# Row sums of the spatial mixing weights: a VectorE reduction with a store and a spreading load in place of a TensorE product with ones

## The chip, the cores and the metric

The kernel runs on one core of one Trainium2 chip. The metric is the device time of one execution in microseconds (us), the median of several. A core has TensorE (PE in the profile; its weight loads are PEld), VectorE (DVE), ScalarE (ACT), GpSimd (POOL) and SyncE (SP), which issues most DMAs. Each works through its own instructions in a fixed order and waits for the others by semaphores.

## The reference, cut to what matters

One layer of a hybrid encoder over 512 tokens of width 1024, all in float32. The part that the change touches is the spatial gating: a layer norm of `zv`, whose gain and bias are `ln_g` and `ln_b`, is mixed over the 128 positions of each chunk by one 128x128 matrix per head.

```
def sgu_branch(zu, zv, ln_g, ln_b, w_s, bias):        # w_s (8, 128, 128), bias (8, 128)
    zu = gelu(zu)
    zv = layer_norm(gelu(zv), ln_g, ln_b)
    zv = zv.reshape(bsz, seq // 128, 128, 8, 128)
    sv = einsum('hts,bnshd->bnthd', w_s, zv) + bias.T[None, None, :, :, None]
    return zu * sv.reshape(bsz, seq, 1024)
```

Beside it run an S5 state-space branch (a scan over 62 chunks of 8 positions, with small products before and after), gates, a cross-attention and a feed-forward network, all with large products.

With z the normalised `zv` before gain and bias, the mixed value of head h, output position t and channel d is `g[d] * (sum over s of w_s[h,t,s] z[s,d]) + b[d] * R[h,t] + bias[h,t]`, where `R[h,t] = sum over s of w_s[h,t,s]` is the row sum of the mixing weights. These row sums are what the change computes in another way.

## The kernel before, in words

Every large product is made exact to about float32 by splitting each operand into a high and a low part (line 85 on ScalarE, `whi`; line 86 on VectorE, `wlo`) and adding three TensorE products (line 374). Weights arrive in blocks of 512 KB (`wraw`, three buffers, issued on SP's queue at line 145), are split into `whi`/`wlo` (three buffers each), and used. A list (`plan`) names all blocks in order: `next_w` hands out one block, splits up to two blocks ahead and loads three ahead.

Side work is threaded between these products. `tick` is called after each block and moves a counter `side["now"]` by about one per 24 matrix products; `later(n, fn)` runs `fn` when the counter has moved by n; the generator `s5_program` gives the S5 branch piece by piece. The program text so made is then put in order for each engine by a scheduler that models durations, so an edit at one place moves neighbours. What is marked `in_order` keeps its program order; `behind(ins, first)` asks that one instruction comes after another, without a wait of its own.

The stage of the change is the one that makes gate a: eight blocks of `w_in` (four calls of `feat` with `ga_evac`, tiles `pf`). Threaded into it are:

- `layer_norm(t)` (lines 1130 to 1142), four times: mean on VectorE (`nm`), squares on ScalarE into the tile `squares`, the factor on GpSimd, the scaling of `zt` on ScalarE.
- the S5 inputs: VectorE makes a factor (lines 972 to 976) in half of the tile `wsx`, TensorE transposes it (`pw`, line 951), ScalarE copies it (`wt`, line 952), TensorE multiplies by `u` (`pz`, line 958), ScalarE and VectorE keep the result in `zh` (lines 963 and 964). The eighth `pz` is the last thing the scan needs before it starts.
- `s5_scan` (lines 985 to 988): 62 steps of four small VectorE instructions each, every step on the one before. After it, lines 1001 and 1002 copy the states into `ss`, and TensorE multiplies them (`py`, line 1014).
- `mixing_setup` (lines 1151 to 1169): TensorE transposes the mixing weights (`wsr`, which were loaded at line 1144) into `pws`, ScalarE copies them into `wst`; gain and bias are transposed into `pgb` and copied into `gbc`; then TensorE multiplies a matrix of ones by `wst` (line 1164), which puts the row sums of every head on all 128 partitions of `prs`, and eight VectorE instructions (line 1167) turn `mix`, which holds the bias, into `R * b + bias`.

After the stage come the mixing products `psv` (line 1191), whose evacuation (line 1192) reads `gbc` and `mix`, and then the blocks of `zu`, of gate b and the products that follow.

`wsx` holds four parts: `wsr`, `wst`, and the two factors of the S5 inputs. `squares` has four rows of 1024 for each partition, one for each token tile.

Of the kernel before, what the change touches and what calls it, by code (L numbers as in the profile page):

```python
# [9 lines left out]
F32 = mybir.dt.float32  # L10
F32R = mybir.dt.float32r
AF = mybir.ActivationFunctionType
ALU = mybir.AluOpType
AX = mybir.AxisListType
# [3 lines left out]
P = 128  # L18
# [11 lines left out]
H = 8  # L30
# [6 lines left out]
OFF_GA = OFF_V + GW  # L37
# [15 lines left out]
def hybrid_layer_kernel(  # L53
# [8 lines left out]
    nc = tc.nc  # L62
# [9 lines left out]
    dp = ctx.enter_context(tc.tile_pool(name="scratch", bufs=1, space=DRAM))  # L72
# [4 lines left out]
    def bank(name):  # L77
        return pm.tile([P, 512], F32, tag="mm", name=name)

    def aux(name, shape=(P, 512)):  # L80
        return pa.tile(list(shape), F32, tag="aux", name=name)
# [35 lines left out]
    def behind(ins, first):  # L117

        tc.add_manual_dep(ins.ins, first.ins.name, mybir.DependencyInfo(
            mybir.DependencyClass.NoSync, mybir.DependencyReason.DATA), reason="order of the casts")  # L120
# [336 lines left out]
    def later(n, fn):  # L457

        side["later"].append((side["now"] + n, fn))
# [32 lines left out]
    ones = cp.tile([P, P], F32, name="ones")  # L492
# [4 lines left out]
    def sum_sq(dst, src, sq=None, bias=0.0):  # L497
        if sq is None:
            sq = np_.tile([P, 512], F32, tag="ev", name="sq", bufs=2)
        act = nc.scalar.activation(sq[:, :src.shape[-1]], src, AF.Square, bias=bias, accum_out=dst)  # L500
        if pinned[0]:
            in_order(act)
# [11 lines left out]
    HALF = (slice(0, 512), slice(512, 1024))  # L514
# [39 lines left out]
    def slot(tag, shape, dt, name, place=NEAR):  # L554
        n = math.prod(shape[1:])
        t = sp.tile([P, KD * T + ROOM[tag]], dt, tag=tag, name=name)[:, place[tag]:place[tag] + n]
        return t.rearrange("p (a b c) -> p a b c", a=shape[1], b=shape[2]) if len(shape) == 4 else (
            t.rearrange("p (a b) -> p a b", a=shape[1]))
# [526 lines left out]
    zsum = cp.tile([P, NT, 2], F32, name="zsum")  # L1085
# [8 lines left out]
    wsr, wst = wsx[:, 0], wsx[:, 1]  # L1094
# [32 lines left out]

    squares = slot("A", (P, NT, GW), F32, "squares")

    def layer_norm(t):  # L1130

        nm, ss, ms, r = (np_.tile([P, 1 + (k == "ss")], F32, tag=k, name=k, bufs=2) for k in ("nm", "ss", "ms", "r"))
        nc.vector.tensor_tensor(nm, zsum[:, t, 0:1], zsum[:, t, 1:2], ALU.add)
        nc.vector.tensor_scalar(nm, nm, -1.0 / GW, None, ALU.mult)
        z = zt[:, t, :]
        for i in range(2):
            sum_sq(ss[:, i:i + 1], z[:, HALF[i]], squares[:, t, HALF[i]], nm)
        nc.vector.tensor_tensor(ms, ss[:, 0:1], ss[:, 1:2], ALU.add)
        nc.vector.tensor_scalar(ms, ms, 1.0 / GW, EPS, ALU.mult, ALU.add)
        nc.gpsimd.tensor_tensor(r, ms, mhalf, ALU.pow)  # L1140
        nc.vector.tensor_tensor(nm, nm, r, ALU.mult)
        nc.scalar.activation(z, z, AF.Identity, bias=nm, scale=r)
# [5 lines left out]
    mix = np_.tile([P, H, P], F32, tag="gain", name="mix", bufs=2)  # L1148
    nc.sync.dma_start(mix, sgu_bias[0].rearrange("h t -> (h t)").partition_broadcast(P))

    def mixing_setup():
        for q in range(2):
            ps = aux("pws", (P, 4, P))
            for j in range(4):
                nc.tensor.transpose(ps[:, j, :], wsr[:, 4 * q + j, :], ident)
            nc.scalar.copy(wst[:, 4 * q:4 * q + 4, :], ps)
        ps = aux("pgb", (P, 2 * H))
        nc.tensor.transpose(ps, gbr, ident[:2 * H, :2 * H])
        gbc = np_.tile([P, 2 * H], F32, tag="gbc", name="gbc", bufs=1)
        nc.vector.tensor_copy(gbc, ps)  # L1160

        for q in range(2):
            ps = aux("prs", (P, 4, P))
            nc.tensor.matmul(ps, ones, wst[:, 4 * q:4 * q + 4, :], start=True, stop=True)
            for j in range(4):
                h_ = 4 * q + j
                nc.vector.scalar_tensor_tensor(mix[:, h_, :], ps[:, j, :], gbc[:, H + h_:H + h_ + 1], mix[:, h_, :],
                                               ALU.mult, ALU.add)
        return gbc

    gad = dp.tile([KD, P, T], F32, name="gad")

    def ga_evac(m, j, ps):
        z = np_.tile([P, T], F32, tag="ev", name="gas", bufs=2)
        nc.scalar.activation(z, ps, AF.Sigmoid)
        nc.sync.dma_start(gad[m - OFF_GA // P], z)

    gbcs = []
    later(5, lambda: gbcs.append(mixing_setup()))
    for i in range(NT):  # L1180
        later(1 + i, lambda i=i: layer_norm(i))
    for c0 in range(OFF_GA, OFF_GB, 256):
        feat(w_in, c0, xn, KD, ga_evac)


    gbc = gbcs[0]
    sv = slot("A", (P, H, T), F32, "sv")
    for h in range(H):
        ps = bank("psv")
# [56 lines left out]
    def unit_bank(name):  # L1246
        return bank(name).rearrange("p (j t) -> p j t", j=2)
# [149 lines left out]
    h = slot("A", (P, NT, D), F32, "h")  # L1397
# [206 lines left out]
    ps = {t: bank(f"pt{t}") for t in range(NT)}  # L1604
# [45 lines left out]
    held, ps = [], {}  # L1650
# [91 lines left out]
    ps = [bank("pf0"), bank("pf1")]  # L1742
# [67 lines left out]
    for i, u in enumerate(UNITS):  # L1810
        final = i == len(UNITS) - 1
        x, v = begun
        q = unit_bank("pq")
# [185 lines left out]
```

## Time and profile before

| what | value |
|---|---|
| median of 3 runs | 866.23 us (866.2, 866.23, 868.49) |
| profiled execution | 865.49 us |
| its span, first to last instruction | 863.7 us |
| mean granted TensorE clock | 0.998 of full speed |
| DMA | 169.56 MB, mean 196 GB/s |

The profiled execution takes 865.49 - 863.7 = 1.79 us more than its span. In the profile a row of a timeline gives start, duration, engine, line, operation, the tile written and the tiles read, how many instructions are merged in the row and, in brackets, how long the engine was idle before it and what ended that. One matrix product in plain float32 (both operands of that type, as `pws`, `prs`, `pz` and `py`) is recorded as two matrix products, so line 1164, which stands twice in the program, shows four.

### The profile page before, as it was taken

The numbers are of one execution on the slowest core, as the hardware profiler recorded it, in microseconds if no ns is written. First come the engines' busy times: TensorE is split into PE (matmuls) and PEld (weight loads), VectorE is DVE, ScalarE is ACT, GpSimd is POOL, SyncE is SP. The second block draws the span as 40 slices with busy tenths as digits, with TensorE's granted clock in tenths as the row PEclk, the third lists the DMA queues.
The fourth block names the chain that finished last, engine by engine and source line by source line (L and its number), as shares of the span: only waits on it lengthen the run. The fifth ranks groups of instructions, "written<-read, shape, count | busy, mean of one in ns | idle before, by whom it ended". The sixth has DMA issues, their size and how long they took to land.

```text
span 863.7 us, 14764 instructions
## 1 busy us (share of the span) xinstructions
PE 856.1 (99%) x5780; PEld 766.6 (89%) x5780; DVE 660.5 (76%) x1076; ACT 466.1 (54%) x698; POOL 89.3 (10%) x119
## 2 busy tenths in 40 slices
PE   9999999999999999999999999999999999999997
PEld 7888888888889988889899888999999999988886
DVE  7698896899846768668758755867877768899875
ACT  6734853244355543557547544645545554656674
POOL 0002302111021110110010001010211111000000
PEclk9999999999999999999999999999999999999999
DMA  9759565987574798735696555557999898366564
GB/s 270 196 174 308 113 174 153 254 195 191 146 220 150 244 309 248 244 102 199 213 276 162 147 146 147 146 159 185 213 233 240 215 229 220 92 191 209 196 186 156
DMA packets 115752, 169.56 MB, mean 196 GB/s; under 512 B 9297, under 2 KB 80481, under 8 KB 115554
## 3 DMA queue, kind: packets, MB, share of 16 engines
q1 hardware_dynamic: 95330, 139.54, 49.3%
q0 software_dynamic: 20064, 28.55, 20.4%
q8 instruction: 45, 0.74, 0.3%
q10 hardware_dynamic: 288, 0.52, 0.2%
q14 instruction: 25, 0.20, 0.1%
HBM read 159.71 MB, written 48.73 MB: 241 GB/s over the span
## 4 chain that ended last, share of the span: by engine, by line
PE 99%; DVE 1%; ACT 0%; issue 0%
PE pf L374 27%; PE pt L374 18%; PE px L1238 13%; PE dx L374 7%; PE pq L1238 6%; PE dq L374 3%; PE pv L1238 3%; PE bx L1238 3%; PE qx L1238 3%; PE dv L374 2%; PE pz L958 2%; PE qv L1238 1%; PE po L374 1%; PE psc L374 1%; PE py L1014 1%; PE qq L1238 1%
## 5 line engine op out<-in xcount | busy, mean ns | idle before, releaser
L85 ACT CAST whi<-wraw 128x1024 fp32r<-128x1024 f32 x141 | 145.2, 1031 | 160.2 <-PE pf L374 54.8
L86 DVE TENSOR_TENSOR wlo<-wraw,whi 128x1024 fp32r<-128x1024 f32 x141 | 168.3, 1195 | 64.8 <-ACT whi L85 64.2
L374 PE MATMUL pf<-xn,whi 128*128 128x512 f32 x448 | 140.1, 392 | 0.0
L374 PEld LDWEIGHTS pf<-xn,whi 128*128 128x128 f32 x448 | 83.5, 188 | 16.9
L374 PE MATMUL pf<-xn,wlo 128*128 128x512 f32 x224 | 87.5, 391 | 0.0
L1238 PE MATMUL px<-fn,whi 128*128 128x256 f32 x480 | 83.4, 277 | 0.0
L1238 PEld LDWEIGHTS px<-fn,whi 128*128 128x128 f32 x480 | 72.5, 188 | 0.2
L86 DVE TENSOR_TENSOR wlo<-b,whi 128x1024 fp32r<-128x1024 f32 x40 | 48.9, 1223 | 26.0 <-ACT whi L85 26.0
L85 ACT CAST whi<-b 128x1024 fp32r<-128x1024 f32 x40 | 42.2, 1054 | 48.3 <-PE px L1238 27.7
L1238 PE MATMUL px<-fn,wlo 128*128 128x256 f32 x240 | 66.4, 277 | 0.0
L1238 PE MATMUL pq<-s,whi 128*128 128x256 f32 x320 | 55.0, 276 | 0.0
L374 PE MATMUL dx<-whi,s 128*128 128x512 f32 x166 | 52.2, 391 | 0.4 <-DVE h L1922 0.4
L86 DVE TENSOR_TENSOR wlo<-t,whi 128x1024 fp32r<-128x1024 f32 x30 | 36.7, 1225 | 18.4 <-ACT whi L85 18.4
L85 ACT CAST whi<-t 128x1024 fp32r<-128x1024 f32 x30 | 31.6, 1054 | 34.6 <-PE pv L1238 11.4
L374 PEld LDWEIGHTS pf<-xn,wlo 128*128 128x128 f32 x224 | 42.1, 188 | 8.7
L1238 PEld LDWEIGHTS pq<-s,whi 128*128 128x128 f32 x320 | 48.2, 188 | 0.0
L1238 PEld LDWEIGHTS px<-fn,wlo 128*128 128x128 f32 x240 | 45.1, 188 | 0.0
L1238 PE MATMUL pq<-s,wlo 128*128 128x256 f32 x160 | 44.2, 276 | 0.0
L374 PE MATMUL pt<-whi,xn 128*128 128x512 f32 x128 | 43.1, 402 | 0.0
L374 PEld LDWEIGHTS dx<-whi,s 128*128 128x128 f32 x166 | 31.1, 188 | 7.4 <-ACT whi L85 0.8
L374 PE MATMUL dx<-wlo,s 128*128 128x512 f32 x83 | 32.2, 389 | 0.0
L289 POOL DMA_DIRECT2D dsum<-in_w_down_dram x12 | 13.2, 1103 | 172.5 <-DMA dsum<-in_w_down_dram 167.4
(458 smaller groups left out, 2222.7 us busy)
## 6 DMA issues: line engine op xcount, KB each, us to landing
wraw<-in_w_in_dram SPq DMA_DIRECT2D x34, 512.0 KB, 4.6
dsum<-in_w_down_dram SPq DMA_DIRECT2D x20, 512.0 KB, 5.8
wraw<-dsum SPq DMA_DIRECT2D x20, 512.0 KB, 4.4
b<-in_w_gate_dram SPq DMA_DIRECT2D x15, 512.0 KB, 5.1
b<-in_w_up_dram SPq DMA_DIRECT2D x15, 512.0 KB, 4.7
wraw<-in_w_down_dram SPq DMA_DIRECT2D x15, 512.0 KB, 3.8
dsum<-in_w_down_dram POOLq DMA_DIRECT2D x10, 512.0 KB, 7.5
dsum<-dsum POOLq DMA_DIRECT2D x10, 512.0 KB, 7.9
```

Source lines behind the costliest of these rows:

```text
L85: hi = nc.scalar.copy(dst_hi, src)
L86: lo = nc.vector.tensor_tensor(dst_lo, src, dst_hi.bitcast(F32), ALU.subtract)
L289: plan[j + step][1].append((0, lambda d=dst, x=more: nc.gpsimd.dma_start(d, x, accum_op=ALU.add)))
L374: m = nc.tensor.matmul(ps, a[x], b[y], start=start and i == 0, stop=stop and i == 2, skip_group_check=free)
L958: nc.tensor.matmul(ps[:, g, :], wt[:, g, :], u[:, o * GO + g, :], start=True, stop=True)
L1014: in_order(nc.tensor.matmul(ps[64 * j:64 * j + 64, :, :, h, :].rearrange("p q d c -> p d q c"), a, b, start=k == ks[0], stop=k == ks[2], t ...
L1238: nc.tensor.matmul(ps[:, j, :], a[x], b[y], start=start and j == k == i == 0, stop=k == 3 and i == 2, skip_group_check=True)
```

## The change

`mixing_setup` no longer multiplies by ones. Instead:

- `row_totals`, due 2.5 ticks into the stage, sums `wsr` (128 partitions of output positions, 8 heads, 128 inputs) over the inputs with one VectorE reduction, into 8 numbers per partition in a free row of `squares`, and stores these 4 KB to a scratch tensor `rsd` in DRAM. The reduction is put behind the second `nm` instruction.
- `spread_totals`, due at 4 ticks, loads the 1024 numbers of `rsd` to every partition (512 KB written), into another free row of `squares` seen as position by head (`rsb`). It is put behind the first store of `gad`.
- the eight instructions that update `mix` read `rsb[:, :, h_]`, a view in SBUF with a step of eight elements, where they read `prs` in PSUM.
- `mixing_setup` is due at 6 ticks, not 5.
- all four `layer_norm` calls write their squares, which nobody reads, into row 0 of `squares`, so that rows 2 and 3 are free.

```
     def layer_norm(t):
 
         nm, ss, ms, r = (np_.tile([P, 1 + (k == "ss")], F32, tag=k, name=k, bufs=2) for k in ("nm", "ss", "ms", "r"))
-        nc.vector.tensor_tensor(nm, zsum[:, t, 0:1], zsum[:, t, 1:2], ALU.add)
+        means.append(nc.vector.tensor_tensor(nm, zsum[:, t, 0:1], zsum[:, t, 1:2], ALU.add))
...
-            sum_sq(ss[:, i:i + 1], z[:, HALF[i]], squares[:, t, HALF[i]], nm)
+            sum_sq(ss[:, i:i + 1], z[:, HALF[i]], squares[:, 0, HALF[i]], nm)
...
-        for q in range(2):
-            ps = aux("prs", (P, 4, P))
-            nc.tensor.matmul(ps, ones, wst[:, 4 * q:4 * q + 4, :], start=True, stop=True)
-            for j in range(4):
-                h_ = 4 * q + j
-                nc.vector.scalar_tensor_tensor(mix[:, h_, :], ps[:, j, :], gbc[:, H + h_:H + h_ + 1], mix[:, h_, :],
-                                               ALU.mult, ALU.add)
+        for h_ in range(H):
+            nc.vector.scalar_tensor_tensor(mix[:, h_, :], rsb[:, :, h_], gbc[:, H + h_:H + h_ + 1], mix[:, h_, :],
+                                           ALU.mult, ALU.add)
         return gbc
+
+    rsd = dp.tile([P, H], F32, name="rsd")
+    rsb = squares[:, 3, :].rearrange("p (t h) -> p t h", h=H)
+
+    def row_totals():
+
+        rs = squares[:, 2, 0:H]
+        behind(nc.vector.tensor_reduce(rs, wsr, AX.X, ALU.add), means[1])
+        nc.sync.dma_start(rsd, rs)
+
+    def spread_totals():
+        behind(nc.sync.dma_start(rsb, rsd.rearrange("t h -> (t h)").partition_broadcast(P)), gads[0])
...
         nc.scalar.activation(z, ps, AF.Sigmoid)
-        nc.sync.dma_start(gad[m - OFF_GA // P], z)
+        gads.append(nc.sync.dma_start(gad[m - OFF_GA // P], z))
 
     gbcs = []
-    later(5, lambda: gbcs.append(mixing_setup()))
+    later(2.5, row_totals)
+    later(4, spread_totals)
+    later(6, lambda: gbcs.append(mixing_setup()))
```

Lines from 1130 on carry new numbers in the changed kernel: 2 more in `layer_norm` and at the start of `mixing_setup`, 12 more after it.

Three places of the order show what moves. The first is TensorE in the gate stage. `pf` are the big products of the gate, `pz` the last product of the S5 inputs, `pk` a small S5 product. Before, around the product with ones:

```order
L374 MATMUL pf_1362<-xn,wlo 128x512
L1164 MATMUL prs<-wsx,ones 128x512 x2
L958 MATMUL pz<-u,wt 128x64 x8
L374 MATMUL pf_1362<-xn,whi 128x512 x2
L374 MATMUL pf_1362<-xn,wlo 128x512
```

In the changed kernel, around the same `pz`:

```order
L374 MATMUL pf_1366<-xn,whi 128x512 x2
L374 MATMUL pf_1366<-xn,wlo 128x512
L958 MATMUL pz<-u,wt 128x64 x8
L374 MATMUL pf_1365<-xn,whi 128x512 x2
L374 MATMUL pf_1365<-xn,wlo 128x512
```

`prs` is gone, and `pz` stands ahead of the transposes `pws` and `pgb`: they follow it by 24 `pf` products, where `pz` followed them by 21 and by `prs`. `pz` is now a group of its own between `pf` products, where it shared one with `prs`. Both kernels have the same 480 big products ahead of `psv`; from there to the first `py` the kernel before has 340 of them, the changed one 323.

The second place is SP's queue, from the last small store `kd` of the third S5 group. In brackets stand the semaphores that an entry waits for (DMAHW are those of earlier DMAs). Before:

```order
L910 DMA kd_873<-ks 16x256 [waits DMAHW6_49]
L145 DMA wraw<-in_w_in_dram 128x4x256 [waits DMAHW7_49,DVE_49]
L145 DMA wraw<-in_w_in_dram 128x4x256 [waits DMAHW0_49,DVE_49]
L145 DMA wraw<-in_w_in_dram 128x4x256 [waits DMAHW1_49,DVE_49]
L1176 DMA gad<-gas 128x512 [waits DMAHW2_49,Activation_49]
L145 DMA wraw<-in_w_in_dram 128x4x256 [waits DMAHW7_49,DMAHW3_49,DVE_49]
```

In the changed kernel:

```order
L910 DMA kd_873<-ks 16x256 [waits DMAHW6_49]
L1176 DMA rsd<-squares 128x8 [waits DMAHW7_49,DVE_49]
L145 DMA wraw<-in_w_in_dram 128x4x256 [waits DMAHW0_49,DVE_49]
L145 DMA wraw<-in_w_in_dram 128x4x256 [waits DMAHW1_49,DVE_49]
L145 DMA wraw<-in_w_in_dram 128x4x256 [waits DMAHW2_49,DVE_49]
L1186 DMA gad<-gas 128x512 [waits DMAHW3_49,Activation_49]
L1179 DMA squares<-rsd 128x1024 [waits DMAHW7_49,DMAHW4_49]
```

The store, which waits for the reduction, stands ahead of three loads of weights; the spreading load stands behind the first store of the gate and waits for the store of the sums.

The third place is VectorE at the update of `mix`. `sa`, `sb` and `zh` on lines 985 to 988 are steps of the scan. Before:

```order
L86 TENSOR_TENSOR wlo<-wraw,whi 128x1024 [waits DMAHW3_49,PE_49,Activation_49]
L1160 COPY gbc<-pgb 128x16 [waits PE_49]
L1167 SCALAR_TENSOR_TENSOR mix<-prs,gbc,mix 128x128 [waits DMAHW6_49,DVE_49,PE_49]
L1167 SCALAR_TENSOR_TENSOR mix<-prs,gbc,mix 128x128 x3
L1167 SCALAR_TENSOR_TENSOR mix<-prs,gbc,mix 128x128 [waits PE_49]
L1167 SCALAR_TENSOR_TENSOR mix<-prs,gbc,mix 128x128 x3
L964 COPY zh<-pz 64x8x64 [waits Activation_49]
L985 TENSOR_TENSOR sa<-zh,ca 128x64 [waits DVE_49]
```

In the changed kernel:

```order
L986 TENSOR_TENSOR sb<-zh,cb 128x64
L86 TENSOR_TENSOR wlo<-wraw,whi 128x1024 [waits DMAHW0_49,PE_49,Activation_49]
L1162 COPY gbc<-pgb 128x16 [waits PE_49]
L899 TENSOR_TENSOR dd<-dmask,dcol 128x32
L987 TENSOR_TENSOR sa<-sa,zh 128x64 [waits DVE_49]
L1165 SCALAR_TENSOR_TENSOR mix<-squares,gbc,mix 128x128 [waits DMAHW6_49,DMAHW4_49,DVE_49]
L1165 SCALAR_TENSOR_TENSOR mix<-squares,gbc,mix 128x128 x7
L988 TENSOR_TENSOR zh<-sa,sb 128x64 [waits DVE_49]
```

The update stood ahead of the last `zh` copy and of the whole scan, and waited for TensorE; it now stands inside the sixth step of the scan and waits for the spreading load. Near the scan's end the changed kernel has one scan instruction between the last `wlo` and the first copy into `ss`, where there were 17.

More of the change, by code (lines that the diff above doesn't have):

```diff
@@ L1128, in hybrid_layer_kernel @@
     squares = slot("A", (P, NT, GW), F32, "squares")
+    means, gads = [], []
     def layer_norm(t):
         nm, ss, ms, r = (np_.tile([P, 1 + (k == "ss")], F32, tag=k, name=k, bufs=2) for k in ("nm", "ss", "ms", "r"))
-        nc.vector.tensor_tensor(nm, zsum[:, t, 0:1], zsum[:, t, 1:2], ALU.add)
+        means.append(nc.vector.tensor_tensor(nm, zsum[:, t, 0:1], zsum[:, t, 1:2], ALU.add))
         nc.vector.tensor_scalar(nm, nm, -1.0 / GW, None, ALU.mult)
```

## The prediction

> **What bounds the kernel now.** I read the first parts of the page, then who waits for whom on TensorE, then the chain of waits around the change. The page first:
>
> ```profile
> span 863.7 us, 14764 instructions
> PE 856.1 (99%) x5780; PEld 766.6 (89%) x5780; DVE 660.5 (76%) x1076; ACT 466.1 (54%) x698; POOL 89.3 (10%) x119
> PE 99%; DVE 1%; ACT 0%; issue 0%
> ```
>
> TensorE is busy for 99% of the span, and 99% of the chain that ended last runs on it. A busy engine may still be held up inside its instructions, so the waits of TensorE come next, and the chain, whose columns are start, duration, engine, tile, line and count:
>
> ```profile
> PE pt L573 <- DVE ones L493: 1.1, 1, 1.1
> PE dx L374 <- DVE h L1922: 0.4, 1, 0.4
> PE ptr L635 <- issue: 0.2, 1, 0.2
> PE ptr L635 <- DVE ms L618: 0.2, 1, 0.2
> ...
> 138.17 1.72 PE prs L1164 x4
> 163.28 36.73 PE pf L374 x162
> ```
>
> TensorE waits 1.9 us in all, 1.1 of it before the first instruction, and never between 76 and 300 us, where the change lies. The last row is the rate: 36.73 / 162 = 0.227 us for each product of 128x512, over 162 of them without a gap, with the clock at full. So the time is the sum of TensorE's work, and every other engine has cover. An edit pays what it takes from TensorE, as long as no cover ends.
>
> The Trainium skill ("Trainium Kernel Development and Optimization", Best Practices) says that the busy time of matrix products is a bad measure of the distance from the bound, since they are pipelined. By that rule the 99% would show nothing, and taking work away could be worth nothing; that is the second rival below. The even 0.227 us speaks against it here.
>
> **What is removed from TensorE.** The timeline of TensorE around the product with ones:
>
> ```profile
> 131.98 1.03 PE L1155 MATMUL pws<-ident,wsx 128*128 128x128 f32 x8
> 132.95 0.23 PE L1158 MATMUL pgb<-ident,gbr 16*128 16x16 f32 x1
> ...
> 138.00 1.88 PE L1164 MATMUL prs<-wsx,ones 128*128 128x512 f32 x4
> 139.72 1.89 PE L958 MATMUL pz<-u,wt 128*128 128x64 f32 x16
> 141.42 0.70 PE L374 MATMUL pf<-xn,whi 128*128 128x512 f32 x2
> 141.97 0.40 PE L374 MATMUL pf<-xn,wlo 128*128 128x512 f32 x1
> 142.20 0.62 PE L374 MATMUL pf<-xn,whi 128*128 128x512 f32 x2
> 142.66 0.39 PE L374 MATMUL pf<-xn,wlo 128*128 128x512 f32 x1
> ```
>
> Durations overlap in the pipeline, so starts are compared. From 138.00 to 139.72 the four recorded products take **1.72 us**; the chain has the same. They go entirely. The order adds one change between small and big products, since `pz` now stands alone. The first pair of big products after `pz` takes 141.97 - 141.42 = 0.55 us, a pair in the stream 142.66 - 142.20 = 0.46. One more such start costs 0.55 - 0.46 = 0.09; I bound it by 0 and 0.3 and take **0.1**. Sum on TensorE: -1.72 + 0.10 = **-1.62 us**. The rest of its list is the same products in a slightly different order, so everything else counts only if TensorE must wait for it.
>
> **The reduction on VectorE.** The only reduction of the trace, the nearest full-width instruction, and the load of VectorE in that stage (columns: PE, PEld, DVE, ACT, POOL busy):
>
> ```profile
> L830 DVE TENSOR_REDUCE dmask<-ident x1: 247/247/247, 2.0 to 2.0; 128x16 f32<-128x64 f32 x1
> ...
> 91.96 1.22 DVE L86 TENSOR_TENSOR wlo<-wraw,whi 128x1024 fp32r<-128x1024 f32 x1
> ...
> 80.00:90.00 10.00, 10.00 (x61) 8.75 (x60) 9.94 (x14) 7.06 (x16) 2.36 (x2) 1.00 1.00 243
> 90.00:100.00 10.00, 10.00 (x68) 9.01 (x66) 9.91 (x17) 7.74 (x13) 2.72 (x2) 1.00 0.66 157
> ...
> 88.72 0.62 PE L374 MATMUL pf<-xn,whi 128*128 128x512 f32 x2
> ...
> 100.05 0.39 PE L374 MATMUL pf<-xn,wlo 128*128 128x512 f32 x1
> ```
>
> It reads 128x1024. The small reduction read a sixteenth of that in 0.25 us: bounds 0.25 and 16 x 0.25 = 4.0 us. I take 1.2, by the row with as many elements. It falls at about 85 us, where VectorE is full (9.94 and 9.91 of 10), so all behind it on VectorE comes 1.2 us later, at worst 4.0. What TensorE needs from there is the low part of the next block of weights: made at 91.96 to 93.18, first used at 100.05 (a block is 24 big products, the stage begins at 88.72, and this is its 27th, the third of its second block). Cover: 100.05 - 93.18 = 6.9 us. So 0; without that cover it would be 1.2.
>
> **The store and the load on SP.** The timeline of SP's queue, and the times from issue to landing (least, median, most) for the load of the bias into `mix`, the gate's stores and the small S5 transfers:
>
> ```profile
> 81.46 2.02 SPq L910 DMA_DIRECT2D kd<-ks  x4
> 93.20 12.48 SPq L145 DMA_DIRECT2D wraw<-in_w_in_dram  x3
> 107.17 0.34 SPq L1176 DMA_DIRECT2D gad<-gas  x1
> ...
> DMA to landing us min/median/max: 5.2/5.2/5.2
> ...
> DMA to landing us min/median/max: 2.0/6.5/15.9
> ...
> DMA to landing us min/median/max: 3.3/5.0/9.2
> ```
>
> The store of 4 KB waits for the reduction, with three loads of weights queued behind it. The reduction ends near 86; the queue stood idle from 83.5 to 93.2 anyhow, since the first of these loads waits for its buffer. Even at 4.0 us the reduction is done by 89: 0. The store lands in 3.3 to 9.2 us, by 98, far ahead of the spreading load, which goes out after the gate's first store at 107.5. Its own issue (0.3 to 0.6 us) delays a later load of weights, which is two blocks early: 0. The spreading load has the form of the load of the bias, 4 KB to 128 partitions, which took 5.2 us: landing at 112.7. The bounds are the gate's stores, 2.0 and 15.9: 109.5 to 123.4. The update that reads it comes after `pgb`: `pz` starts at 131.98 in the new order (all ahead of it is the same work), takes 141.42 - 139.72 = 1.70, then 24 products of 0.227, then `pws` in 0.97, so not before 140.1. Cover 16.7 us: 0.
>
> **The update and the scan on VectorE.** Before, VectorE stood for TensorE at the update:
>
> ```profile
> 139.06 2.16 DVE L1167 SCALAR_TENSOR_TENSOR mix<-prs,gbc,mix 128x128 f32<-128x128 f32 x8 [4.38 <-PE prs L1164]
> 142.75 1.09 DVE L964 COPY zh<-pz 64x512 f32<-64x512 f32 x1 [1.53 <-ACT zh L963]
> ```
>
> The wait of 4.38 us goes, and the scan, which starts after the last `zh` copy, starts earlier by 139.72 - 131.98 = 7.7 us. The eight updates, 2.16 us, now stand inside it, so its lead is 5.6 us. TensorE draws on that lead, because `py` is moved ahead. The end of the scan, its copies and `py`:
>
> ```profile
> 229.48 1.23 DVE L86 TENSOR_TENSOR wlo<-wraw,whi 128x1024 fp32r<-128x1024 f32 x1 [0.60 <-ACT whi L85]
> 230.62 0.22 DVE L988 TENSOR_TENSOR zh<-sa,sb 128x64 f32<-128x64 f32 x1
> ...
> 233.77 0.23 DVE L988 TENSOR_TENSOR zh<-sa,sb 128x64 f32<-128x64 f32 x1
> 234.03 2.09 DVE L1002 COPY ss<-zh 64x1008 f32<-64x1008 f32 x2
> ...
> 234.78 3.94 ACT L1001 COPY ss<-zh 64x1008 f32<-64x1008 f32 x2
> ...
> 240.30 0.66 PE L1014 MATMUL py<-e,ss 128*64 128x128 f32 x8
> ```
>
> Before, the first ScalarE copy ends at 234.78 + 1.97 = 236.75, and `py` starts 3.55 us later. In the new order `py` is 17 big products earlier, 3.85 us, and the removal moves it by 1.72 more: it is due at 234.7. The scan has four steps fewer after the last `wlo`, (233.77 - 230.62) = 3.15 us, and that `wlo` follows TensorE, 1.72 earlier: 4.87 us are needed, 5.6 are there. The cover stays at 3.5 us, and 0.7 behind it: I price this at 0. For the updates the operand is no longer PSUM but SBUF with a step of 32 bytes. The `ss` copy on line 1002 reads `zh` with a step of 256 bytes and takes 1.05 us for 1008 elements, about 1 ns each, so a step costs nothing there: bounds 1.0 us for all eight and, with a doubling, 4.3; I keep 2.16.
>
> The Trainium skill ("SBUF — State Buffer", Door 1: The DMA port swizzle) says that SBUF lines have 16 bytes and that each access that crosses to a new line pays a penalty, in float32 any step over 4. By that rule the updates get dearer, by an amount that it doesn't give; at twice the time the scan would still be inside its cover, and the sum stays. The copy on line 1002 speaks against it.
>
> **The sum.** 865.49 - 1.62 = 863.9 for an execution like the profiled one. The median of the runs is 866.23, 0.74 higher: 866.23 - 1.62 = **864.6 us**, 0.19% faster. About 0.3%, 2.6 us, is what a measurement of this kernel can tell from no change, so this counts as no change (863.6 to 868.8). The forecast's own range is 864.3 to 865.5.
>
> **The rivals.**
> 1. *TensorE waits for the scan* (slower). Place: the first `py`, due at 234.7. The scan must end by 232.0, so that a copy of 1.97 us and the 0.75 us ahead of it fit. For it: VectorE is full from 80 to 100 us, the updates stand in the scan, and the lead of 5.6 us may be eaten by `wlo` casts that wait for TensorE. If the scan ends as before at 234.0, TensorE waits 2.0 us and the time is 866.6. If it ends 2.2 us later still, by the updates, the wait is 4.2 and the time 868.8; with some loss in the loads behind it 869.5. It decides from a scan end of 232.0 on and makes the kernel slower by over 0.3% from 236.2 on. Against it: 3.5 us of cover and a lead that suffices by the rows. Chance 0.16.
> 2. *The change does not do what it says*: the removed products filled time in which TensorE would have waited anyway, or a wait of 1 to 2 us appears at another place. Then 866.2. Against it: no wait on TensorE from 76 to 300 us. Chance 0.12.
> 3. *The wait of 4.38 us on VectorE counted*: it held work that TensorE only seemed not to miss, and the gain is the sum of both, 1.62 + up to 4.4, so 861 to 863.5. Against it: TensorE never waited behind it. Chance 0.07.
>
> **How the numbers follow.** Forecast 0.65, rivals 0.16, 0.12, 0.07. The forecast and rival 2 lie within 0.3%, with a fifth of rival 1 (scan ends between 232 and 236): 0.65 + 0.12 + 0.03 = 0.80, less 0.02 for scatter of the runs to the fast side. Faster 0.09, same 0.78, slower 0.13. The range must reach rival 2 and the milder half of rival 1 above, and the edge of rival 3 below: 863.3 to 867.8.
>
> **What would show it.** In the changed profile `prs` is missing and TensorE's busy time is about 1.6 us less; its waits name nothing new between 80 and 300 us; the span is near 862.1; the reduction takes 1.0 to 1.4 us; the spreading load lands before 124 us and the first update of `mix` waits for no DMA; the scan ends near 229 us and `py` starts near 234.7. A wait of TensorE on `ss` at `py`, or on `wlo` between 95 and 120 us, would make the prediction wrong on the slow side; an update of `mix` above 4 us or a landing after 140 us would be the first sign of it.

## The result, and the profile after

| what | before | after |
|---|---|---|
| median of 20 runs each | 867.51 us (865.68 to 870.25) | 865.64 us (863.65 to 869.01) |
| ratio, 95% interval | 1 | 0.9977 [0.9969, 0.9986] |
| profiled execution, its span | 865.49 us, 863.7 | 865.88 us, 864.1 |

The change takes 0.23% off, 2.0 us of 867.5, with an interval of 1.2 to 2.7 us. That lies within the 0.3% that the prediction counted as no change, though the interval excludes zero. The two profiled executions say the opposite: the changed one is 0.4 us longer. But the profiled execution before, 865.49 us, is faster than every one of the 20 timed runs of its kernel, while the one after lies near the median of its own. So the pair has to be compared stage by stage. First the head of the page after, and who waits for whom on TensorE:

```profile
span 864.1 us, 14763 instructions
PE 855.3 (99%) x5776; PEld 766.1 (89%) x5776; DVE 662.2 (77%) x1077; ACT 465.9 (54%) x698; POOL 88.4 (10%) x119
...
PE ptr L534 <- ACT full L540: 1.2, 1, 1.2
PE pt L573 <- DVE ones L493: 1.1, 1, 1.1
PE dx L374 <- DVE h L1934: 0.4, 1, 0.4
```

Four TensorE instructions are gone. TensorE's busy time fell by 856.1 - 855.3 = 0.8 us, not by 1.7, since `pg`, shown next, took 1 us longer. Between 80 and 300 us TensorE still waits for nothing. One wait is new, 1.2 us at a `ptr` on line 534, but it stands near 530 us.

The chain of waits of the changed kernel (start, duration, engine, tile, line, count):

```profile
3.99 2.93 PE pg L608 x4
...
121.31 1.15 PE pf L374 x5
...
133.24 1.73 PE pz L958 x16
134.97 5.53 PE pf L374 x24
140.51 0.87 PE pws L1157 x8
...
155.52 7.15 PE psv L1203 x64
162.67 73.22 PE pf L374 x323
235.89 5.39 PE py L1014 x96
...
256.29 2.77 PE py L1014 x48
```

The same places in the chain of the kernel before:

```profile
3.99 1.94 PE pg L608 x4
...
120.20 1.15 PE pf L374 x5
...
156.14 7.14 PE psv L1191 x64
...
256.82 2.77 PE py L1014 x48
```

The reader is to take differences of starts. At 121 us, ahead of the removed products, the changed execution is 121.31 - 120.20 = 1.11 us late. It loses 0.99 us at `pg`, four products at 4 us that the change does not touch, 2.93 us long here and 1.94 there; the last section says why. By 82 us 0.82 of that is left, and around `pw`, the transpose that ends at 84.93 here and at 83.87 there, it loses another 0.24. Both places stand ahead of the reduction, which starts at 86.1. At `psv` it is 156.14 - 155.52 = 0.62 us early, so the stage of the change gained 1.11 + 0.62 = 1.73 us. At the third group of `py`, where both kernels have done the same work, it is 0.53 early: 1.11 + 0.53 = 1.64 us in all. The 1.2 us at `ptr` is lost 270 us further on. So the profiled pair holds the gain of 1.64 us, and against it 2.3 us of losses that stand outside the stage of the change: 1.11 ahead of it and 1.2 behind.

The side work that replaced the products: the reduction, the store and the spreading load in the changed kernel (least, median and most in ns, then first and last start), then the time from issue to landing, and the row of the updates in the timeline of VectorE:

```profile
L1175 DVE TENSOR_REDUCE squares<-wsx x1: 1217/1217/1217, 86.1 to 86.1; 128x8 f32<-128x1024 f32 x1
...
L1176 SPq DMA_DIRECT2D rsd<-squares x1: 348/348/348, 87.3 to 87.3; - x1
L1179 SPq DMA_DIRECT2D squares<-rsd x1: 384/384/384, 109.1 to 109.1; - x1
...
DMA to landing us min/median/max: 5.4/5.4/5.4
...
143.06 3.02 DVE L1165 SCALAR_TENSOR_TENSOR mix<-squares,gbc,mix 128x128 f32<-128x128 f32 x8
```

The landing time is that of the 4 KB store; this view has none for the spreading load, but the trace's record of single DMA packets has it. On SP's queue 128 packets of 4096 bytes, one for each partition, run from 110.16 to 113.12 us. They are the only ones of that size between 81 and 231 us, and the kernel before has none there. So the load, which went out at 109.1, was in place some 30 us ahead of the updates, which start at 143.06 without idle time ahead of them. The updates take 3.02 us where they took 2.16.

The end of the scan and the first `py` in the changed kernel:

```profile
228.86 1.22 DVE L86 TENSOR_TENSOR wlo<-wraw,whi 128x1024 fp32r<-128x1024 f32 x1 [0.60 <-ACT whi L85]
230.00 0.22 DVE L988 TENSOR_TENSOR zh<-sa,sb 128x64 f32<-128x64 f32 x1
230.25 3.90 ACT L1001 COPY ss<-zh 64x1008 f32<-64x1008 f32 x2 [1.43 <-DVE zh L988]
235.82 0.66 PE L1014 MATMUL py<-e,ss 128*64 128x128 f32 x8
```

The first of the two ScalarE copies ends at 230.25 + 1.95 = 232.2, and `py` starts 3.6 us later. Ahead of the last `wlo` VectorE was idle for 0.60 us, until ScalarE had made the high part, as before the change (0.60 there too): the scan was not late.

### The profile page after: what moved, and what is told of

The parts are those of the page before. It is cut to its first block, busy times and chain, and to the rows that moved or that the text cites. A ratio compares the mean times of both kernels' runs of the same rounds, so it can differ in the third digit from the quotient of the medians.

```text
span 864.1 us, 14763 instructions
## 1 busy us (share of the span) xinstructions
PE 855.3 (99%) x5776; PEld 766.1 (89%) x5776; DVE 662.2 (77%) x1077; ACT 465.9 (54%) x698; POOL 88.4 (10%) x119
## 4 chain that ended last, share of the span: by engine, by line
PE 96%; DVE 1%; DMA 1%; issue 0%; ACT 0%; POOL 0%; SPq 0%; POOLq 0%; ACTq 0%
PE pf L374 27%; PE pt L374 15%; PE px L1250 13%; PE dx L374 7%; PE pq L1250 6%; PE dq L374 3%; PE pv L1250 3%; PE bx L1250 3%; PE qx L1250 3%; PE dv L374 2%; PE pz L958 2%; PE qv L1250 1%; PE po L374 1%; PE psc L374 1%; PE py L1014 1%; PE qq L1250 1%
```

## The experiments

The theory: TensorE's time is a sum, the four removed products are the whole gain, and the detour over VectorE, SP and DRAM is hidden, at last by 3.6 us of cover at `py`. The rivals: the gain comes from the order (the moved `pz`, the set-up that is due later); the detour costs something, so that the gain could be larger; the cover is smaller than it looks. Each experiment has 4 to 12 runs. The first four were timed beside the kernel before at 867.76 us (20 runs), the next four at 867.32 us (21 runs), the last at 866.95 us (16 runs).

**The products with ones back, everything else as changed** (`e1_ones_kept`).

```
         gbc = np_.tile([P, 2 * H], F32, tag="gbc", name="gbc", bufs=1)
         nc.vector.tensor_copy(gbc, ps)
+        for q in range(2):
+            ps = aux("prs", (P, 4, P))
+            nc.tensor.matmul(ps, ones, wst[:, 4 * q:4 * q + 4, :], start=True, stop=True)
         for h_ in range(H):
```

> The changed kernel with the two products with ones put back on TensorE at the end of the mixing set-up; nobody reads what they give. Theory (TensorE sets the time, the gain is the 1.72 us of these products): all of the gain is gone, ratio to the kernel before 1.000, some 1.7 us above the changed kernel, and no new wait on TensorE. Rival (the gain is VectorE's wait of 4.4 us, or the new order): the time stays at the changed kernel's, ratio about 0.998.

Measured: 867.38 us, ratio 1.000 [0.9991, 1.0009]. The gain is gone. Two rows of its chain:

```profile
147.99 1.72 PE prs L1166 x4
...
158.25 7.15 PE psv L1206 x64
```

The products stand in the chain with the same 1.72 us as before, though in another place and read by nobody. One new wait of TensorE was not expected: 0.7 us for VectorE at a `pw`, which starts at 84.88 us. It stands ahead of the gate, and `e2_no_row_sums`, which has no detour, has 0.5 us of it too.

**The products gone, no detour** (`e2_no_row_sums`), from the kernel before.

```
-            ps = aux("prs", (P, 4, P))
-            nc.tensor.matmul(ps, ones, wst[:, 4 * q:4 * q + 4, :], start=True, stop=True)
             for j in range(4):
                 h_ = 4 * q + j
-                nc.vector.scalar_tensor_tensor(mix[:, h_, :], ps[:, j, :], gbc[:, H + h_:H + h_ + 1], mix[:, h_, :],
+                nc.vector.scalar_tensor_tensor(mix[:, h_, :], wst[:, h_, :], gbc[:, H + h_:H + h_ + 1], mix[:, h_, :],
                                                ALU.mult, ALU.add)
```

> The kernel before without the row sums: the products with ones are left out, nothing takes their place, and the update of mix reads the transposed weights instead, so the bias term is not the reference's. Theory (store, load and reduction cost nothing, since they are covered): the same time as the changed kernel, ratio 0.998 to the kernel before. Rival (the detour by DRAM and the reduction cost part of what the products took): faster than the changed kernel by what they cost, 1 us or more, ratio 0.9965 or less.

Measured: 864.94 us, ratio 0.9976 [0.9964, 0.9988], the change's own ratio to 0.0001. The reduction, the store, the load and the dearer updates cost nothing that these runs can measure; the two intervals leave about 1.3 us either way, and the traces, compared below, far less. Its updates read SBUF without a step:

```profile
L1165 DVE SCALAR_TENSOR_TENSOR mix<-wsx,gbc,mix x8: 347/348/352, 136.7 to 138.6; 128x128 f32<-128x128 f32 x8
```

**The sums stored by head, so that the updates read without a step** (`e3_heads_first`).

```
-    rsd = dp.tile([P, H], F32, name="rsd")
-    rsb = squares[:, 3, :].rearrange("p (t h) -> p t h", h=H)
+    rsd = dp.tile([H, P], F32, name="rsd")
+    rsb = squares[:, 3, :].rearrange("p (h t) -> p h t", h=H)
...
-        nc.sync.dma_start(rsd, rs)
+        nc.sync.dma_start(rsd.rearrange("h t -> t h"), rs)
...
-        behind(nc.sync.dma_start(rsb, rsd.rearrange("t h -> (t h)").partition_broadcast(P)), gads[0])
+        behind(nc.sync.dma_start(rsb, rsd.rearrange("h t -> (h t)").partition_broadcast(P)), gads[0])
...
-            nc.vector.scalar_tensor_tensor(mix[:, h_, :], rsb[:, :, h_], gbc[:, H + h_:H + h_ + 1], mix[:, h_, :],
+            nc.vector.scalar_tensor_tensor(mix[:, h_, :], rsb[:, h_, :], gbc[:, H + h_:H + h_ + 1], mix[:, h_, :],
```

> The changed kernel with the sums stored by head and then position, so that the update of mix reads 128 neighbouring elements and not every eighth; the order of every engine is that of the changed kernel. If the step of 32 bytes is what makes an update take 0.45 us where it took 0.34 with PSUM: the update falls to 0.34 us or less. If it is the operand in SBUF as such: it stays at 0.45. In both cases the time stays at the changed kernel's, ratio 0.998, since the scan has cover; a gain of 0.8 us or more would say that the scan was on the path.

Measured: 865.03 us, ratio 0.9967 [0.9955, 0.9979], no different from the change. One update of `mix` with the step, in the changed kernel:

```profile
L1165 DVE SCALAR_TENSOR_TENSOR mix<-squares,gbc,mix x8: 444/449/460, 143.1 to 145.6; 128x128 f32<-128x128 f32 x8
```

and without it, in this run:

```profile
L1165 DVE SCALAR_TENSOR_TENSOR mix<-squares,gbc,mix x8: 347/348/350, 143.4 to 145.3; 128x128 f32<-128x128 f32 x8
```

The same data from the same tile, in the same order of instructions: the step of 32 bytes costs 449 - 348 = 101 ns for each update of 128 elements, 0.8 ns an element. Reading SBUF in place of PSUM costs 348 - 342 = 6 ns; 342 is the median of the eight updates before the change. The eight updates together cost 0.8 us more, hidden in the scan.

**The set-up due at 5 ticks, as before the change** (`e4_set_up_at_5`): `later(5, ...)` in place of `later(6, ...)`.

> The changed kernel with the mixing set-up due at 5 ticks as before, not 6, so that the order of transposes, last S5 product and scan is again that of the kernel before, without the products with ones. Theory: the same time as the changed kernel, ratio 0.998, since neither order makes TensorE wait. Rival (the later set-up and the earlier scan are part of the gain): 0.5 us or more slower than the changed kernel.

Measured: 865.0 us, ratio 0.9971 [0.9959, 0.9982]. The order is then again like that of the kernel before, with the set-up ahead of the last `pz`, and the time is that of the change. So the moved `pz` is no part of the gain.

The traces of these runs say the same more finely. The table has starts in each run's chain of waits, in us: the first `pf` of the gate, the first `psv`, and the differences from there on.

| | before | after | `e1_ones_kept` | `e2_no_row_sums` | `e3_heads_first` | `e4_set_up_at_5` |
|---|---|---|---|---|---|---|
| first `pf` of the gate | 88.89 | 89.97 | 90.97 | 90.42 | 90.34 | 89.99 |
| first `psv` | 156.14 | 155.52 | 158.25 | 155.96 | 155.90 | 155.55 |
| the gate stage | 67.25 | 65.55 | 67.28 | 65.54 | 65.56 | 65.56 |
| first `psv` to third `py` | 100.68 | 100.77 | 101.14 | 100.67 | 100.77 | 100.68 |

With the products the stage takes 67.25 and 67.28 us, without them 65.54 to 65.56, whatever the detour and the order. So the products are worth 1.70 us there, and the detour costs 0.02 at most. Behind `psv` the changed kernel loses 0.09 us, which is gone where the set-up is due at 5 ticks again: that is the price of its moved order.

**How far the cover reaches.** Five runs draw on the cover. The first two only move the first `py` ahead in TensorE's order, by an order-only dependency (N = 14 in the first, 2 in the second):

```
+            if first_py:
+                first_py.append(m)
+                if len(first_py) == N:
+                    behind(m, first_py[0])
```

Here `m` is each big product that the program gives after the first group of `py`, whose last product is `first_py[0]`. The other three add work that nobody reads to the set-up, behind the updates (K = 8, 8 and 3), with N = 14 in the first and third of them and the order left alone in the second:

```
+        for _ in range(K):
+            nc.vector.scalar_tensor_tensor(squares[:, 1, :], wsr.rearrange("p h s -> p (h s)"), gbc[:, 0:1], wst.rearrange("p h s -> p (h s)"), ALU.mult, ALU.add)
```

> The changed kernel with the first `py` products moved ahead by 11 big products in TensorE's order (794 of them ahead of it, where the changed kernel has 805); no work is added. In the changed kernel the scan's first copy on ScalarE ends at 232.2 and `py` starts at 235.8, so the cover is 3.6 us. Theory (the cover is as the profile shows it): 11 x 0.227 = 2.5 us of it are used, 1.1 us stay, TensorE has no wait at `py`, median 864.5 to 866 us, as the changed kernel. Rival (the cover is smaller than it looks, since the copies or the scan depend on TensorE's own progress): a wait of TensorE on the copies of line 1001 of up to 2.5 us, median up to 868 us.

> The changed kernel with the first `py` products moved ahead by 35 big products (770 ahead of it), which is 7.9 us; no work is added. Theory: the cover of 3.6 us is used up, TensorE waits 7.9 - 3.6 = 4.3 us for the copies behind the scan, the wait stands in the profile at the first `py`, and the median is 4.3 us above the changed kernel, 869 to 870.5 us. This is the first rival of the prediction, brought about on purpose. Rival (the wait lets other engines catch up and is given back later): median within 1.5 us of the changed kernel's, 864.5 to 867 us, though the wait stands in the profile.

> As the run with 794 big products ahead of the first `py`, and eight full-width VectorE instructions (128x1024, result unread) behind the updates of `mix`, inside the scan. At 1.2 us each (the casts of the same size take 1.22) they put off the scan's end by 9.8 us. Theory: the cover left is 1.1 us, TensorE waits 9.8 - 1.1 = 8.7 us at `py`, median 873 to 875 us. Rival (VectorE has idle time of its own in the scan that takes them in): a wait under 3 us, median below 868 us.

> The changed kernel with the same eight full-width VectorE instructions inside the scan, and the order left to itself: the first `py` then stands behind 842 big products, 37 later, 8.4 us. Theory: cover 3.6 + 8.4 = 12.0 us against 9.8 us of added work, so TensorE does not wait and the median is as the changed kernel's, 864.5 to 866.5 us: VectorE's work costs nothing as long as the order gives it cover. Rival (work on VectorE in the scan costs by itself, through the casts or the clock): median 869 to 875 us, as in the run with `py` early.

> As the run with eight added VectorE instructions and the first `py` behind 794 big products, with three of them: 3 x 1.29 = 3.9 us later at the scan's end, 1.1 us of cover, so TensorE waits 2.8 us at `py`. In the two runs that waited 4.3 and 6.7 us the granted clock fell to 0.50 some 4 us after TensorE went idle, and the 48 recorded `py` products took 4.31 and 4.99 us in place of 2.77. Theory (the clock falls only when the wait lasts about 4 us): a wait of 2.8 us leaves the clock at 1.00, `py` takes 2.77 us, and the median is 2.8 us above the run without added work, about 868.1 us. Rival (any wait costs a restart): `py` takes 4.0 us or more in place of 2.77, median 869.3 us or more.

The number of big products ahead of the first `py` is counted in the traces here, where the changed kernel has 803; the expectations count two more in every run.

| run | first `py` behind | added to the scan | median us | ratio, 95% interval | TensorE waits at `py` |
|---|---|---|---|---|---|
| `e5_py_early` | 792 | none | 865.32 | 0.9976 [0.9965, 0.9987] | 0 |
| `e9_scan_loaded_little` | 792 | 3 x 1.29 us | 868.19 | 1.0012 [1.0001, 1.0023] | 2.0 us |
| `e6_py_earlier` | 768 | none | 872.29 | 1.0058 [1.0044, 1.0072] | 4.3 us |
| `e7_scan_loaded` | 792 | 8 x 1.29 us | 875.27 | 1.009 [1.0076, 1.0104] | 6.7 us |
| `e8_scan_loaded_py_late` | 840 | 8 x 1.27 us | 865.45 | 0.9981 [0.9972, 0.9989] | 0 |

The cover is real, and has the size that was read from the profile. Without added work and 2.5 us earlier, `py` waits for nothing. With `py` 7.9 us earlier TensorE waits 4.3 us, the 7.9 - 3.6 that was worked out; its waits in `e6_py_earlier`:

```profile
PE py L1019 <- DVE ss L1007: 4.3, 1, 4.3
```

With 8 x 1.27 = 10.2 us of VectorE work added and the order left alone, `py` moves back 37 products, TensorE does not wait at `py`, and the time is that of the change. The work is not quite free: TensorE waits elsewhere, in the mixing products, for VectorE's evacuation of them:

```profile
PE psv L1205 <- DVE sv L1206: 0.4, 1, 0.4
```

By the third group of `py` this execution has lost 0.6 us on the changed kernel (123.63 us from the last `pz` on, against 123.05), which the medians, 865.45 and 865.64, do not resolve.

With work added, the waits at `py` came out shorter than expected: 2.0 us where 2.8 was expected and 6.7 where it was 8.7. In `e9_scan_loaded_little` the copies of line 1001 start 3.2 us later than in the changed kernel (233.44 against 230.25) for 3.9 us of work, so idle time of VectorE took in some 0.7, as the rival of `e7_scan_loaded` had it, though far less than that rival needs. In `e7_scan_loaded` TensorE was itself 1.8 us later at that point: it goes idle at 235.0, where `py` starts at 233.2 in `e5_py_early`. The median of `e7_scan_loaded`, 875.27, is above the 873 to 875 that were expected all the same, for the reason that comes next.

The price of a wait was not as expected. The median of `e6_py_earlier` is 7.0 us above `e5_py_early`, not 4.3. The chain of `e5_py_early`, at the first and the third group of `py`:

```profile
233.20 2.77 PE py L1019 x48
...
256.47 2.77 PE py L1019 x48
```

The same two places in `e6_py_earlier`:

```profile
232.13 4.31 PE py L1019 x48
...
262.39 2.77 PE py L1019 x48
```

The first 48 products after the wait took 4.31 us in place of 2.77, 1.54 us more. With the wait that makes 4.3 + 1.5 = 5.8 us, and at the third group this execution is 262.39 - 256.47 = 5.92 us behind, 0.1 of which it had from the start. Why they are slower stands in the table of stretches of `e6_py_earlier` (in each row: stretch, its length, busy time of TensorE, of its weight loads, VectorE, ScalarE and GpSimd with counts, then the granted clock, the DMA share and GB/s):

```profile
230.00:231.00 1.00, 0.00 (x0) 0.00 (x0) 0.96 (x2) 0.86 (x1) 0.00 (x0) 1.00 0.06 12
231.00:232.00 1.00, 0.00 (x0) 0.00 (x0) 1.00 (x2) 1.00 (x2) 0.00 (x0) 0.89 0.96 303
232.00:233.00 1.00, 0.87 (x8) 0.90 (x10) 0.10 (x1) 1.00 (x2) 0.00 (x0) 0.50 0.53 209
...
234.00:235.00 1.00, 1.00 (x14) 1.00 (x12) 0.00 (x0) 0.84 (x2) 0.00 (x0) 0.50 0.00 0
235.00:236.00 1.00, 1.00 (x20) 1.00 (x18) 0.00 (x0) 0.00 (x0) 0.00 (x0) 0.91 0.00 0
```

TensorE's last product ended at 227.9. The granted clock falls to half at about 231.8, 3.9 us later, just before the copies are done, and is back at full at about 235.2, when TensorE has worked for 3 us. Half of the clock for 3.0 us costs 1.5 us. With the wait of 6.7 us the fall came 4.4 us after the last product, and the chain has the first 48 at 4.99 us:

```profile
241.73 4.99 PE py L1019 x48
```

`e9_scan_loaded_little` was run to see whether any wait costs this; its chain:

```profile
235.42 2.84 PE py L1019 x48
...
258.76 2.77 PE py L1019 x48
```

After a wait of 2.0 us they take 2.84 us, the clock stays at 1.00 throughout, and the loss at the third group is 258.76 - 256.47 = 2.3 us, 2.2 of it the later start of `py` (235.42 - 233.20). So in these profiled executions the wait of 2.0 us costs hardly more than itself, and the one of 4.3 us costs itself and 1.5 us more. By the ratios of the runs the first costs about 3.1 us (1.0012 - 0.9976) and the second 7.1, each with 1.4 us either way.

The Trainium skill ("TensorE: Matmul & The Clock Gate", Part 1: The HAM clock gate) says that the array runs at half its clock after an idle window of about 3.4 us, that it needs about as long a busy window to get the full clock back, and that the windows run freely, so that the moment varies. The traces, in their record of the granted clock, agree on the length and the free run: the half clock lasts from 231.78 to 235.19 us in `e6_py_earlier`, 3.41 us, and from 239.35 to 246.18 in `e7_scan_loaded`, 6.83 us or twice that, and in every trace the stretch between two changes of the clock is a whole multiple of 3.41 us. They differ in one point: here the window need not be idle throughout. At the end of the 11 kernels the clock falls between 2.4 and 5.2 us after TensorE's last product; in `e9_scan_loaded_little` it falls 2.4 us after it, when TensorE had worked for 1.0 us of the last 3.41. In the same run's wait at `py` it had worked for 1.5 us of the window that holds most of the wait, 231.89 to 235.30 us by these steps, and the clock stayed. So 2.0 us is not shown to be safe at every moment; one trace shows that it was safe here.

Two things stay open. The medians of `e6_py_earlier` and `e5_py_early` differ by 7.0 us, their profiles by 5.8 at the third `py`. The profiled execution of the one is the fastest of its five runs (871.11 us), that of the other is 1.0 us above its median, and the two ratios leave about 1.4 us either way, so this may be scatter; no run settles it. And no run made the spreading load late: it lands some 30 us before it is read, and where a later landing begins to cost was not tried.

## Why the prediction was right, point by point

- **What bounds the kernel.** Right. With the products put back the gain vanishes, and with the detour taken away nothing more is gained. Rival 2, that the busy share says nothing and the removed products filled idle time, falls with the first of these. The rule of the Trainium skill that stood beside it ("Trainium Kernel Development and Optimization", Best Practices) did not decide here: TensorE's busy time was made of work that had to be done, and taking 1.72 us of it away paid.
- **The time itself.** 865.64 us lies in the range of 863.3 to 867.8, but 1.0 us above the forecast of 864.6, just outside the forecast's own 864.3 to 865.5, and nearer to the 866.2 of rival 2. The base was off: 866.23 us by 3 runs, 867.51 by 20. What held is the difference, and the absolute time alone could not have told the forecast from rival 2; `e1_ones_kept` and `e2_no_row_sums` do.
- **The removed products and the one more switch**, -1.72 and +0.10. The stage gained 1.73 us up to `psv`, and 1.64 remained at the third `py`; forecast -1.62. The runs' 2.0 us [1.2, 2.7] holds it. The 0.10 was put in the wrong place: the switch at `pz` costs 0.02 at most, and 0.09 is lost behind `psv`, by the moved order. That the sum came out is partly luck.
- **The reduction**, 1.2 us: 1.217 measured. The row with as many elements was the right neighbour; the small reduction, scaled by 16, would have given 4.0.
- **The store and the spreading load.** The store landed in 5.4 us (3.3 to 9.2 were the bounds). The spreading load was forecast to land at 112.7 and its last packet ends at 113.1; the updates waited for no DMA, not even in `e4_set_up_at_5`, where they start at 136.2 and the last packet ends at 113.0. The cost is 0, as forecast.
- **The update of `mix`**, kept at 2.16 us: 3.02 measured. This term was mis-sized, inside its bounds of 1.0 to 4.3. The step that failed is "a step costs nothing", taken from a copy that runs at 1 ns an element with a step of 256 bytes. That row had no partner without a step to compare it with, so it could not show what a step costs. `e3_heads_first` is that partner for the updates: 449 ns with the step, 348 without. The rule of the Trainium skill that the prediction set against the copy ("SBUF — State Buffer", Door 1: The DMA port swizzle) had the direction right; it gives no amount, and the runs add one, 0.8 ns an element.
- **The scan's lead and the cover at `py`.** 5.6 us of lead and 3.5 us of cover were forecast. The updates were 0.9 us dearer, which by the sum left 4.7 us of lead against 4.87 needed; VectorE's idle 0.60 us ahead of the last `wlo` shows that there was still some to spare, and the cover came out at 3.6 us. `py` started at 235.82; forecast 234.7, and 1.1 of late start-up.
- **Rival 1**, TensorE waits for the scan. It did not come about, but it is the right danger, and was brought about: a wait of 4.3 us, close to the 4.2 that the prediction priced at 868.8 to 869.5, which is 4.2 to 4.9 above its forecast. It cost 5.8 us in the trace and 7.0 by the medians; what the price left out is the clock's fall, 1.5 us. The trace of before has such a fall only at its end, from 861.05 us on, 3.0 us after TensorE's last product, where nothing is left to slow down.
- **Rival 3**, VectorE's wait of 4.38 us counts. It would have added up to 4.4 us to the gain. The stage shows 1.73 and no more.
- **The signs in the profile.** No wait is new between 80 and 300 us, the reduction and the landing are as forecast, and the scan ends at 230.2 us, the forecast's 229 and the late start-up. The span near 862.1 did not show: 864.1, by the 1.1 us ahead of the stage and the 1.2 us at `ptr`. Nor did 1.6 us less of busy time: 0.8, by the 1 us at `pg`.

## What to carry to other kernels

On an engine that is busy without a gap, removing an instruction pays its start-to-start time, and what replaces it on other engines is free as long as it ends within its cover, which is to be named and measured: here 3.6 us at `py`. Look at two profiles by differences at common points of their chains, not by their spans; here about 1 us ahead of the stage and 1.2 us far behind it hid a gain of 1.64. And price a new wait on TensorE with the clock that comes after it: here 2.0 us cost 2.3 us in the trace, and 4.3 us cost 5.8, and by the runs both may cost about 1 us more.

## What the runs showed of the hardware that was not expected

- A step of 32 bytes in one SBUF operand of a VectorE instruction costs 0.10 us for 128 float32 elements, 0.449 against 0.348 us.
- TensorE's granted clock falls to 0.50 when TensorE goes idle: 3.9 and 4.4 us after its last product in the two long waits, 2.4 to 5.2 us after it at the end of the 11 kernels. The stretches between its changes are whole multiples of 3.41 us. After the waits the first 48 recorded `py` products took 4.31 and 4.99 us in place of 2.77.
- The start of an execution varies with the same clock. The first four products `pg` took 1.94 us in the profiled execution of the kernel before, 2.93 in the changed one and 3.11 in `e4_set_up_at_5`. The trace's record of the granted clock begins at 4.31, 6.29 and 6.67 us in these three; ahead of it the table of stretches prints 1.00 because nothing is recorded. The rows speak for half the clock there: in the kernel before, `pt` takes 0.24 us a product at first and 0.11 later:

```profile
1.06 2.93 PE pt L573 x12
...
5.93 0.45 PE pt L573 x4
```

If `pg`, which starts at 3.99 us and has 1.72 us of work by the four products of `prs`, ran at half the clock up to the first record, it would take 1.88, 2.87 and 3.06 us, each 0.05 or 0.06 less than measured. So the 0.99 us by which the changed execution is late at `pg` fits the moment at which its clock was released, and nothing that the change does.

- The wait of 1.2 us at `ptr`, near 530 us, stands in the profiles of the changed kernel, `e1_ones_kept`, `e2_no_row_sums`, `e5_py_early` and `e9_scan_loaded_little`, with 1.0 us in `e3_heads_first`, 0.4 in `e6_py_earlier` and 0.2 in `e8_scan_loaded_py_late`; it is missing in those of the kernel before, `e4_set_up_at_5` and `e7_scan_loaded`. `e1_ones_kept` has the detour and not the gain, `e2_no_row_sums` the gain and not the detour, and `e4_set_up_at_5` both, so the wait follows neither. With one profile of each kernel its cause stays open.
